# An encoder layer on one core: other landing buffers for the prompt's stored gates and the sample's merged sums, and the eps of the query and key norm as a 65th column

## The chip, the core and the metric

The kernel runs on one core of one Trainium2 chip. The metric is the device time of one execution in microseconds (us). The engines are named as in the profile: PE is TensorE's matrix multiply (PEld its weight load), DVE is VectorE, ACT is ScalarE, POOL is GpSimd, SP is SyncE, from whose queue every transfer of this kernel is issued.

## The reference

One layer of an encoder is applied to two batches with the same weights: a prompt of 512 tokens and a sample of 1024 tokens, 1024 channels each, in float32.

```python
h = rmsnorm(x, norm_g)
qa, ka, va, za, qb, kb, vb, zb, ga, gb = split(h @ w_in)
qa, ka = rmsnorm(qa, qn_a), rmsnorm(ka, kn_a)      # over the 64 of a head
oa = neighbourhood_attention(qa, ka, va, rpb_a) * silu(za)
oa = oa @ w_o_a
qb, kb = rmsnorm(qb, qn_b), rmsnorm(kb, kn_b)
ob = window_gqa_attention(qb, kb, vb, t5_table, sink_b) * silu(zb)
ob = ob @ w_o_b
merged = sigmoid(ga) * oa + sigmoid(gb) * ob
return x + merged @ w_out
```

rmsnorm divides by the root of (mean of squares + eps), with eps 1e-6. Branch A attends on a grid of rows of 64 tokens, branch B in a band of 128 tokens with two key heads, a bias table and a sink.

## The kernel before

**Numbers.** Float32 operands are split into a high part (rounded by ACT, L1172, L605, L665) and a low part (the rest, by DVE or POOL, L1177, L610). A product is three matmuls: high by high, low by high, high by low (L1293, L1294, L1295; in the projection all three at L764). The page calls the parts hh and hl (of h), whi and wlo (of weights), T (of sums), fh and fl (of the weights of filling products).

**Stages.** Each batch passes through `attention_phase` and then `dense_phase`; the profile shows the prompt's attention up to some 220 us, its dense part to 390, the sample's attention to 790, its dense part to the end. In the attention, `project` (L737 and on) multiplies one block of 128 tokens by 384 columns of the input weights, for six groups of columns, 24 matmuls each. Then follows the norm of queries and keys, one chain per product: ACT squares (`sq`, L783), DVE sums over the 64 of each head (`ss`, L788), POOL multiplies by 1/64 and adds eps (`rs_v`, L795), POOL raises to the power -1/2 (`rs_r`, L802), DVE or ACT multiply (`qk`, L819, L669, L665), and PE transposes the result (L864) for the scores (L937). Behind the scores, DVE takes the maximum (L972), ACT the exponential (L981), DVE or POOL the division by the sum (`sb`, L1013 and L1011), PE transposes (L1029) and multiplies by the values (L1066).

`fill_gates` (L1590 and on) gives PE products of the merge gates that can be made at any time of the attention, in the bank "d"; they are the filling products. Their weights land in `fr`, their parts are `fh` and `fl`.

In the dense part the output gates z, the rest of the merge gates, the two branch products and the output product follow. Where it pays, two products share sums of blocks, so that seven products of half size do for eight. For the sample, such sums of h are stored to `t_d`, and such sums of the merged values to `m_d` (`merged_sums`, L1705); `stored_sums` (L1237 to L1253) loads them again (L1245) and splits them into T. The merge loop (L1708 to L1747) makes the branch products, loads the stored gates `g_d` (L1729), multiplies and adds. `pairs_apart` (L1419 to L1505) makes the sample's output product: of every pair it first copies the products that only need h-like operands out of the bank (`leave`, L1440), and later adds those with T.

**Memory.** A landing buffer is a value with a tag; a tag has a number of buffers that are used in turn. For this change: U has 4, ot 2, raw 4, C 4 for the prompt and 5 for the sample, sq 1, and the spare tags fh, fl, fr and w32 (on the page w) 2 each, fc 1.

**What sets the order.** Class `Flow` is a list scheduler that runs when the program is built. Each operation has one or more engines with modelled times, a priority, the operations that it comes after, and the values that it makes or holds. `Flow.run` goes through modelled time, gives each engine the ready operation of the lowest priority number whose buffers are free, and writes the instructions out in that order. For the tags whi, wlo, w32, T, S, raw, U, C and ot a buffer is only given in the order in which the program names its values. On the chip each engine then runs its own list, in that order, with semaphores between engines; SP issues the transfers in its order too, and one that waits for its buffer holds those behind it. So a change of one operation, a buffer or a modelled time moves other instructions as well.

## Time and profile before

| | |
|---|---|
| three runs | 1139.26 us median (1133.87, 1139.26, 1140.91) |
| the profiled execution | 1139.25 us, its span from the first to the last instruction 1137.5 us |
| mean granted clock of TensorE | 0.998 |
| matmuls and transposes | 6079 |
| moved by DMA | 186.11 MB, mean 164 GB/s |
| DVE instructions, POOL instructions | 1988, 438 |

A row of a timeline gives the start in the span, the duration, the engine, the line, the operation, out<-in, and in brackets how long the engine was idle before it and what ended that. A row of the waits gives the engine and line that waited, what it waited for, the total, how often, and the longest. A row of the chain gives the start, the length and what ran, followed back from the last instruction. A window's row gives the busy time of PE, PEld, DVE, ACT and POOL with the number of their instructions, then the granted clock, the DMA engines' busy share and GB/s. Starts of matmuls follow each other faster than their durations, since they are pipelined.

### The profile page before, as it was taken

The page shows a single profiled execution, that of the slowest core. Times are in us where ns is not written, and L with a number is a line of the kernel's source. Part 1 is how long each engine was busy: PE and PEld are TensorE (multiplying, and loading weights), DVE is VectorE, ACT ScalarE, POOL GpSimd, SP SyncE. Part 2 cuts the span into 40 slices and gives each one's busy share as a digit, 9 for nine tenths or more (in the row PEclk, how much of TensorE's full clock was granted, in tenths as well). Part 3 has the DMA queues.
Part 4 walks back from the last instruction along what each step waited for, and adds up shares of the span by engine and source line. Part 5 has one row for each costly group of instructions (what it writes and reads, how often), then busy time and mean ns, then how long its engine had stood idle before and what let it go on. Part 6 is the DMA issues. An engine that isn't in the chain of part 4 may idle for free.

```text
span 1137.5 us, 18703 instructions
## 1 busy us (share of the span) xinstructions
PE 1121.8 (99%) x6079; PEld 975.1 (86%) x6079; DVE 856.8 (75%) x1988; ACT 651.4 (57%) x1499; POOL 339.3 (30%) x438
## 2 busy tenths in 40 slices
PE   8999999999999999999999999999999999999998
PEld 6999988888888889999999988988788888888877
DVE  5878797587776568787878889876988766767564
ACT  5777987644532247565769888877543435333430
POOL 3654433000011144434324343510333323123111
PEclk9999999999999999999999999999999999999999
DMA  7854543488785743121213214244888645756862
GB/s 257 273 159 138 185 115 103 107 254 257 246 286 202 249 138 91 29 61 29 82 41 93 73 38 119 50 131 138 288 261 237 206 158 191 278 197 224 262 208 93
DMA packets 139108, 186.11 MB, mean 164 GB/s; under 512 B 29897, under 2 KB 68561, under 8 KB 139010
## 3 DMA queue, kind: packets, MB, share of 16 engines
q1 hardware_dynamic: 139010, 184.91, 51.8%
q8 instruction: 48, 0.79, 0.3%
q14 instruction: 50, 0.41, 0.1%
HBM read 137.66 MB, written 51.92 MB: 167 GB/s over the span
## 4 chain that ended last, share of the span: by engine, by line
PE 90%; DMA 4%; DVE 2%; ACT 1%; issue 1%; SPq 1%; POOL 0%; ACTq 0%; DVEq 0%
PE p L764 26%; PE x L1293 8%; PE x L1295 8%; PE x L1294 8%; PE x L1066 5%; PE x L1029 5%; PE x L937 5%; PE p L1294 4%; PE p L1295 4%; PE p L1293 4%; PE d L1293 4%; PE d L1295 4%; PE d L1294 4%; PE x L864 2%; DMA w<-in_w_att_dram 1%; DMA U<-m_d 1%
## 5 line engine op out<-in xcount | busy, mean ns | idle before, releaser
L764 PE MATMUL p<-whi,hh 128*128 128x384 f32 x384 | 133.7, 348 | 0.0
L764 PE MATMUL p<-whi,hl 128*128 128x384 f32 x384 | 132.6, 345 | 0.0
L764 PE MATMUL p<-wlo,hh 128*128 128x384 f32 x384 | 132.0, 344 | 0.0
L1172 ACT ACTIVATE whi<-raw 128x512 fp32r<-128x512 f32 (+1 forms) x140 | 81.5, 600 | 73.0 <-PE x L1294 22.5
L981 ACT ACTIVATE sb<-sb,mx 128x384 f32<-128x384 f32 (+1 forms) x192 | 107.7, 565 | 16.9 <-DVE mx L972 16.6
L1294 PE MATMUL x<-T,whi 128*128 128x512 f32 x280 | 108.9, 389 | 0.0
L1293 PE MATMUL x<-T,whi 128*128 128x512 f32 x280 | 108.9, 389 | 0.0
L1295 PE MATMUL x<-T,wlo 128*128 128x512 f32 x280 | 108.9, 389 | 0.0
L764 PE MATMUL p<-whi,hb 128*128 128x384 f32 x384 | 107.6, 346 | 0.0
L1177 DVE TENSOR_TENSOR wlo<-raw,whi 128x512 fp32r<-128x512 f32 (+1 forms) x110 | 73.4, 678 | 34.5 <-ACT whi L1172 31.0
L1177 POOL TENSOR_TENSOR wlo<-raw,whi 128x512 fp32r<-128x512 f32 (+1 forms) x30 | 36.4, 1219 | 210.2 <-ACT whi L1172 210.2
L1040 DVE TENSOR_TENSOR pp<-x,pp 128x512 fp32r<-128x512 f32 (+1 forms) x136 | 82.6, 639 | 19.2 <-ACT pp L1035 18.5
L802 POOL TENSOR_TENSOR rs_r<-rs_v,mhalf 128x4 f32<-128x4 f32 (+1 forms) x72 | 80.7, 1121 | 5.7
L1293 PE MATMUL x<-hh,whi 128*128 128x512 f32 x200 | 78.4, 392 | 2.1 <-ACT fh L1440 2.1
L1035 ACT ACTIVATE pp<-x 128x512 fp32r<-128x512 f32 (+1 forms) x136 | 70.9, 561 | 15.2 <-PE x L1029 14.0
L1295 PE MATMUL x<-hh,wlo 128*128 128x512 f32 x200 | 78.5, 393 | 0.0
L1294 PE MATMUL x<-hl,whi 128*128 128x512 f32 x200 | 78.3, 392 | 0.0
L1066 PE MATMUL x<-pp,v 128*128 128x256 f32 (+1 forms) x368 | 75.8, 322 | 0.0
L764 PEld LDWEIGHTS p<-whi,hl 128*128 128x128 f32 x384 | 72.8, 190 | 1.3 <-issue 1.0
L764 PEld LDWEIGHTS p<-wlo,hh 128*128 128x128 f32 x384 | 73.0, 190 | 1.0 <-issue 0.7
L764 PEld LDWEIGHTS p<-whi,hh 128*128 128x128 f32 x384 | 73.0, 190 | 0.7 <-DVE v L812 0.3
L764 PEld LDWEIGHTS p<-whi,hb 128*128 128x128 f32 x384 | 69.1, 188 | 3.0 <-issue 1.3
(388 smaller groups left out, 2967.8 us busy)
## 6 DMA issues: line engine op xcount, KB each, us to landing
raw<-in_w_g_dram SPq DMA_DIRECT2D x84, 256.0 KB
w<-in_w_att_dram SPq DMA_DIRECT2D x46, 384.0 KB
raw<-in_w_z_dram SPq DMA_DIRECT2D x40, 256.0 KB
ot<-o_d SPq DMA_DIRECT2D x36, 256.0 KB
g_d<-C SPq DMA_DIRECT2D x34, 256.0 KB
fr<-in_w_g_dram SPq DMA_DIRECT2D x28, 256.0 KB
raw<-in_w_out_dram SPq DMA_DIRECT2D x28, 256.0 KB
out_dram<-C SPq DMA_DIRECT2D x19, 256.0 KB
```

The costliest lines, as they stand in the source:

```text
L764: pe.matmul(ps.t[:, :GW], part[u](k), mv.t[:, c], start=k == 0 and m == 0, stop=k == KC - 1 and m == 2,)
L802: lambda e: nc.gpsimd.tensor_tensor(r.t[:, :nn], rv.t[:, :nn], mhalf[:, :nn], op=ALU.pow),
L937: pe.matmul(pss[2 * pair + i].t[:, :width], q.t[rows, u, at : at + P], kv[:, tiles[0] : tiles[-1] + 1 : step], start=n == 0, stop=n == 2,)
L981: act.activation(sb.t[:, :width], sb.t[:, :width], AF.Exp, bias=mx.t[:, i : i + 1], scale=-1.0, accum_out=sm.t[:, i : i + 1],)
L1035: lambda e, pt=pt, pp=pp, nn=nn: act.activation(pp.t[:, 0, :nn], pt.t[:, :nn], AF.Copy),
L1040: lambda e, pt=pt, pp=pp, nn=nn: dve.tensor_tensor(pp.t[:, 1, :nn], pt.t[:, :nn], pp.t[:, 0, :nn].bitcast(F32), op=ALU.subtract),
L1066: pe.matmul(out(), v.t[:, vs], mv(), start=first, stop=last)
L1172: (("act", ACT_(n)),), lambda e: act.activation(hi(), src(), AF.Copy), prio,
L1177: lambda e: engines[e].tensor_tensor(lo(), src(), hi().bitcast(F32), op=ALU.subtract), prio,
L1293: pe.matmul(out, hi.t[:, cs], mh(), start=first and k == 0, stop=False, **more)
L1294: pe.matmul(out, hi.t[:, cs], ml(), start=False, stop=False, **more)
L1295: pe.matmul(out, lo.t[:, cs], mh(), start=False, stop=last and k == len(ws) - 1, **more)
```

## The change

Three edits. First, the tile `sq` is made once per attention phase with 65 columns for each head; POOL writes eps to the 65th column once (L673 of the changed kernel), ACT squares with a scale of 0.125 (0.125 squared is 1/64) into the first 64, DVE sums over 65, and POOL's multiply and add (`rs_v`) is gone: the power takes `ss`. Second, in `stored_sums` the sums of the merged values land in U for even blocks and in ot for odd ones, where all landed in U; those of `t_d` land as before. Third, in the prompt's merge loop the stored gates of branch B land in fh or fl by turns, not in ot, and their transfers come after an earlier product of the loop, or after the sixth last product that reads h.

```diff
@@ -668,6 +668,9 @@
             else:
                 engines[e].tensor_scalar(out, in_, scale, None, op0=ALU.mult)
 
+        sq = tile_([P, 336], F32, "sq", 1)
+        sqv = lambda n: sq.t[:, : n * 65].rearrange("p (h d) -> p h d", d=65)
+        sq_ops = [f.op((("pool", 100),), lambda e: nc.gpsimd.memset(sqv(5)[:, :, 64:], EPS), -0.5, new=[sq])]
         a_tables = geo.tables()
         at = np.cumsum([0, *(n for n, _ in a_tables)]).tolist()
         mask = tile_([P, at[-1]], F32, "mask", 1)
@@ -773,34 +776,25 @@
                         kw["after"].append(done[u, k // 4])
                     o = f.op((("pe", PE_(GW)),), emit, prio, use=[mv], hold=[held[u][k]], **kw)
                     f.begun.setdefault((nt, prio), o)
-            sq = tile_([P, 320], F32, "sq", 1)
             ss = tile_([P, 8], F32, "ss", 2)
-            rv = tile_([P, 8], F32, "rs_v", 2)
             r = tile_([P, 8], F32, "rs_r", 2)
             v = tile_([P, 256], F32R, "v", 7 if nt == NT_S else 6)
             f.op(
                 (("act", ACT_(nn * 64, False)),),
-                lambda e: act.activation(sq.t[:, : nn * 64], ps.t[:, : nn * 64], AF.Square),
-                prio, new=[sq], use=[ps],
-            )
-            f.op(
-                (("dve", DVE_(nn * 64)),),
-                lambda e: dve.tensor_reduce(
-                    ss.t[:, :nn], sq.t[:, : nn * 64].rearrange("p (h d) -> p h d", d=64), axis=AX.X, op=ALU.add
+                lambda e: act.activation(
+                    sqv(nn)[:, :, :64], ps.t[:, : nn * 64].rearrange("p (h d) -> p h d", d=64), AF.Square, scale=0.125
                 ),
-                prio, new=[ss], use=[sq],
-            )
-            f.op(
-                (("pool", 165),),
-                lambda e: nc.gpsimd.tensor_scalar(
-                    rv.t[:, :nn], ss.t[:, :nn], 1.0 / 64, EPS, op0=ALU.mult, op1=ALU.add
-                ),
-                prio, new=[rv], use=[ss],
-            )
+                prio, use=[ps], hold=[sq], after=sq_ops[-1:],
+            )
+            sq_ops.append(f.op(
+                (("dve", DVE_(nn * 65)),),
+                lambda e: dve.tensor_reduce(ss.t[:, :nn], sqv(nn), axis=AX.X, op=ALU.add),
+                prio, new=[ss], hold=[sq], after=f.ops[-1:],
+            ))
             f.op(
                 (("pool", 1000),),
-                lambda e: nc.gpsimd.tensor_tensor(r.t[:, :nn], rv.t[:, :nn], mhalf[:, :nn], op=ALU.pow),
-                prio, new=[r], use=[rv],
+                lambda e: nc.gpsimd.tensor_tensor(r.t[:, :nn], ss.t[:, :nn], mhalf[:, :nn], op=ALU.pow),
+                prio, new=[r], use=[ss],
             )
             nv = GW - nn * 64
 
@@ -1240,7 +1234,7 @@
                 tv[j] = tuple(f.value(tp, [P, 4, nh], F32R, "T", 8) for _ in range(2))
                 vh, vl = tv[j]
                 for k in range(4):
-                    st = spare(("fh", "w32")[k // 2]) if not short and d is t_d and k % 2 else tile_("U", 4)
+                    st = tile_("U", 4) if k % 2 == 0 else spare(("fh", "w32")[k // 2]) if d is t_d else tile_("ot", n_ot)
                     dma(
                         lambda st=st, j=j, k=k: nc.sync.dma_start(st.t[:, :nh], d[j, k]), 512 * nh, prio, new=[st],
                         after=[*after(j, k), *([opened] if d is t_d else [])],
@@ -1705,6 +1699,7 @@
                     lambda vd=vd, j=j: nc.sync.dma_start(m_d[j, k], vd.t), 512 * sn, prio, after=[o], hold=[vd],
                 )
 
+        gates_end = h_reads[-6]
         for q in range(8):
             m = q if short else q // 2 + 4 * (q % 2)
             prio = 12 + q
@@ -1723,8 +1718,11 @@
                     ]
                     m_done[q, n] = product(ps, ws[br], movs, prio, True, True)
                     tag, bufs = (("C", n_c), ("ot", n_ot) if short else ("U", 4))[br]
-                    g = tile_(tag, bufs) if short or br or m < 4 else spare("fl" if n else "fh")
-                    turn = [] if short or br or m < 4 else [m_done[max(q - 2, 0), 0]]
+                    g = spare(("fh", "fl")[m % 2]) if br and short else tile_(tag, bufs) if short or br or m < 4 else spare("fl" if n else "fh")
+                    if short:
+                        turn = [m_done[m - 3, 0] if m > 3 else gates_end] if br else []
+                    else:
+                        turn = [] if br or m < 4 else [m_done[max(q - 2, 0), 0]]
                     dma(
                         lambda g=g, br=br, m=m, n=n: nc.sync.dma_start(g.t, g_d[br, m, :, half[n]]), 512 * nh,
                         prio - 0.5, new=[g], after=[*stores["g", br, m, n], *turn],
```

What the scheduler makes of it, engine by engine, follows at three places (lines of the changed kernel are 2 to 6 lower behind the edits: L1245 is L1239, L1177 is L1171, L802 is L796).

**The sample's merged sums, SP.** Transfers at the end of the sample's branch products and the start of its output product. U and ot are landing buffers, raw holds weights (in_w_out) or stored sums of weights (s_d), C an input or output block. Before:

```order
L1430 DMA raw<-s_d 128x512
L1257 DMA raw<-in_w_out_dram 128x512
L1245 DMA U<-m_d 128x512 x4
L1569 DMA C<-in_xt_s_dram 128x512
L1245 DMA U<-m_d 128x512
L1430 DMA raw<-s_d 128x512
L1583 DMA out_dram<-C 128x512
L1245 DMA U<-m_d 128x512 x3
L1430 DMA raw<-s_d 128x512
L1569 DMA C<-in_xt_s_dram 128x512
L1430 DMA raw<-s_d 128x512
L1245 DMA U<-m_d 128x512 x4
```

In the changed kernel, around the last three stores of m_d:

```order
L1239 DMA U<-m_d 128x512
L1424 DMA raw<-s_d 128x512
L1239 DMA U<-m_d 128x512
L1424 DMA raw<-s_d 128x512
L1239 DMA U<-m_d 128x512 x2
L1699 DMA m_d<-C 128x512
L1699 DMA m_d<-fl 128x512
L1563 DMA C<-in_xt_s_dram 128x512
L1699 DMA m_d<-fh 128x512
L1239 DMA U<-m_d 128x512
```

and some rows further:

```order
L1239 DMA ot<-m_d 128x512
L1251 DMA raw<-in_w_out_dram 128x512
L1239 DMA ot<-m_d 128x512
L1563 DMA C<-in_xt_s_dram 128x512
L1424 DMA raw<-s_d 128x512
L1577 DMA out_dram<-C 128x512
L1424 DMA raw<-s_d 128x512
L1239 DMA ot<-m_d 128x512
L1424 DMA raw<-s_d 128x512
L1239 DMA ot<-m_d 128x512
L1563 DMA C<-in_xt_s_dram 128x512
L1239 DMA ot<-m_d 128x512
```

Before, three loads of m_d stand ahead of its last stores and thirteen behind them. Now eight in U are issued ahead of the last stores or right behind them, one in ot earlier still, and seven in ot later, one by one among other transfers.

**The same place, ACT.** L1440 (now L1434) copies a product out of its bank. Before:

```order
L1440 ACTIVATE fh<-x 128x512
L1172 ACTIVATE T<-U 128x512 x4
L1172 ACTIVATE whi<-raw 128x512 x2
L1172 ACTIVATE whi<-raw 128x256
L1172 ACTIVATE T<-U 128x512 x3
L1440 ACTIVATE fh<-x 128x512
L1172 ACTIVATE T<-U 128x512 x2
```

In the changed kernel:

```order
L1434 ACTIVATE fh<-x 128x512
L1166 ACTIVATE T<-ot 128x512
L1166 ACTIVATE whi<-raw 128x512
L1166 ACTIVATE T<-ot 128x512
L1166 ACTIVATE whi<-raw 128x512
L1166 ACTIVATE whi<-raw 128x256
L1166 ACTIVATE T<-ot 128x512
L1434 ACTIVATE fh<-x 128x512
L1166 ACTIVATE T<-ot 128x512 x2
```

Between the last two copies stood seven splits of sums; three stand there now, the third right ahead of the last copy: it is the split of the fifth of the seven late landings in ot.

**The start of the sample's attention, POOL.** raw<-raw is the end of the prompt's dense part. Before:

```order
L1177 TENSOR_TENSOR wlo<-raw,whi 128x512 x4
L1166 TENSOR_TENSOR raw<-raw 128x512 x4
L1177 TENSOR_TENSOR fl<-fr,fh 128x512
L795 TENSOR_SCALAR rs_v<-ss 128x4
L802 TENSOR_TENSOR rs_r<-rs_v,mhalf 128x4
L795 TENSOR_SCALAR rs_v<-ss 128x4
L802 TENSOR_TENSOR rs_r<-rs_v,mhalf 128x4
L698 TENSOR_TENSOR bias<-mask,raw 128x16x8
```

In the changed kernel:

```order
L1160 TENSOR_TENSOR raw<-raw 128x512
L673 MEMSET sq 128x5
L1160 TENSOR_TENSOR raw<-raw 128x512 x3
L1171 TENSOR_TENSOR fl<-fr,fh 128x512
L796 TENSOR_TENSOR rs_r<-ss,mhalf 128x4 x2
L701 TENSOR_TENSOR bias<-mask,raw 128x16x8
```

The powers stand in the place of the multiply and add, behind the same low part. On PE, six matmuls of filling products (d<-hh,fh and its like) stand there between the projection's matmuls and the first transposes L864, now L858, where nine stood. In the whole program 16 more of the divisions by the sum (L1011) go to POOL.

**The seam between the sample's attention and its dense part, SP.** u_d is the store of gated values, o_d that of attention's output. Before:

```order
L1520 DMA u_d_94<-C 128x512
L1535 DMA ot<-o_d_80 128x8x64 x2
L1520 DMA u_d_94<-C 128x512
L1257 DMA raw<-in_w_z_dram 128x512
L1245 DMA U<-t_d 128x512
L1245 DMA fh<-t_d 128x512
L1245 DMA U<-t_d 128x512
L1257 DMA raw<-in_w_z_dram 128x512
L1245 DMA w_10639<-t_d 128x512
```

In the changed kernel:

```order
L1514 DMA u_d_94<-C 128x512
L1251 DMA raw<-in_w_z_dram 128x512
L1529 DMA ot<-o_d_80 128x8x64
L1251 DMA raw<-in_w_z_dram 128x512 x2
L1239 DMA U<-t_d 128x512
L1239 DMA w_10368<-t_d 128x512
L1239 DMA U<-t_d 128x512
L1239 DMA fh<-t_d 128x512
L1239 DMA U<-t_d 128x512
L1239 DMA w_10392<-t_d 128x512
L1529 DMA ot<-o_d_80 128x8x64
L1514 DMA u_d_94<-C 128x512
```

Six loads of t_d now stand in a row ahead of a store of u_d that stood among them. On PE, 15 more matmuls of filling products stand at the end of the sample's attention, and the first products with T come in whole groups of twelve where they were mixed by threes.

More of the change, by code (lines that the diff above doesn't have):

```diff
@@ L782, in project @@
                 (("act", ACT_(nn * 64, False)),),
[L783 to L799 removed]
+                lambda e: act.activation(
+                    sqv(nn)[:, :, :64], ps.t[:, : nn * 64].rearrange("p (h d) -> p h d", d=64), AF.Square, scale=0.125
+                ),
+                prio, use=[ps], hold=[sq], after=sq_ops[-1:],
+            )
+            sq_ops.append(f.op(
[3 more added lines that the diff above has]
+            ))
             f.op(
                 (("pool", 1000),),
[L802 to L803 removed]
+                lambda e: nc.gpsimd.tensor_tensor(r.t[:, :nn], ss.t[:, :nn], mhalf[:, :nn], op=ALU.pow),
+                prio, new=[r], use=[ss],
             )
```

1 line of the change is left out of this document (removed).

## The prediction

> **What bounds the kernel now.** I read the shares of the engines first, then TensorE's own waits, then windows of 20 us, and last the timeline around each wait.
>
> ```profile
> PE 1121.8 (99%) x6079; PEld 975.1 (86%) x6079; DVE 856.8 (75%) x1988; ACT 651.4 (57%) x1499; POOL 339.3 (30%) x438
> ...
> PE x L1807 <- DMA rb<-in_norm_row_dram: 4.6, 1, 4.6
> PE x L864 <- DVE qk L819: 2.4, 2, 1.9
> PE x L1293 <- ACT fh L1440: 2.1, 1, 2.1
> PE d L1294 <- DVE T L1177: 1.3, 1, 1.3
> ...
> PE p L1294 <- DVE T L1177: 0.2, 1, 0.2
> ```
>
> TensorE is busy for 99% of the span, and no edit takes a matmul away. So an edit can win only what lies between matmuls, or what a lowered clock costs. The list of waits (total, times, longest) is short, and it is the whole stock: the first row is the start of the program, which the change doesn't touch; the other four name the places that the edits can reach.
>
> ```profile
> 220.00:240.00 20.00, 20.00 (x90) 16.54 (x89) 9.28 (x21) 9.21 (x15) 0.00 (x0) 1.00 0.82 245
> 800.00:820.00 20.00, 18.49 (x80) 14.63 (x79) 19.03 (x26) 11.00 (x21) 6.22 (x5) 1.00 0.97 320
> 1080.00:1100.00 20.00, 17.91 (x73) 14.30 (x72) 12.95 (x22) 8.15 (x16) 3.12 (x4) 0.91 0.61 202
> ```
>
> The windows (PE, PEld, DVE, ACT, POOL, each with its instructions, then granted clock, DMA share, GB/s) say the same by place. The prompt's dense part is full. Two windows of the sample's dense part are not: 80 and 73 matmuls where the full one has 90. In the second the mean clock is 0.91.
>
> **The sample's merged sums.** This is the largest term. TensorE's rows around the wait, and the clock behind it:
>
> ```profile
> 1083.27 0.39 PE L1294 MATMUL d<-hl,whi 128*128 128x512 f32 x1
> 1083.50 0.39 PE L1295 MATMUL d<-hh,wlo 128*128 128x512 f32 x1
> 1085.98 0.50 PE L1293 MATMUL x<-hh,whi 128*128 128x512 f32 x1 [2.09 <-ACT fh L1440]
> ...
> 1083.50:1087.10 3.60, 1.51 (x7) 0.94 (x6) 2.12 (x5) 1.64 (x3) 0.00 (x0) 1.00 0.78 290
> 1087.10:1090.50 3.40, 3.40 (x10) 2.67 (x9) 2.31 (x6) 1.90 (x4) 0.00 (x0) 0.52 0.24 90
> ```
>
> From start to start it is 2.48 us, where the matmuls ahead of it follow each other by 0.23: the wait costs 2.25. Then, for 3.40 us, the granted clock is 0.52, which costs 3.40 x 0.48 = 1.6. Together 3.9 us hang on this one place. What ends it is ScalarE's copy L1440, which frees the bank, and that copy stood in ScalarE's queue behind a split of a merged sum:
>
> ```profile
> 1065.07 4.92 DMA U<-m_d
> 1070.01 0.64 ACT T L1172
> ...
> 1074.04 4.59 DMA U<-m_d
> ...
> 1080.04 4.75 DMA U<-m_d
> 1084.83 0.51 issue
> 1085.34 0.59 ACT fh L1440
> ...
> 1088.06 0.63 ACT L1172 ACTIVATE T<-U 128x512 fp32r<-128x512 f32 x1 [1.61 <-DMA U<-m_d]
> ```
>
> The chain of waits shows three rounds of landings, one behind the other, on four buffers U (the last row, from ScalarE's timeline, is the split of the last one). In SyncE's queue the reuse of a U buffer shows directly:
>
> ```profile
> 1065.07 1.91 SPq L1245 DMA_DIRECT2D U<-m_d  x4
> ...
> 1071.39 0.32 SPq L1245 DMA_DIRECT2D U<-m_d  x1
> ```
>
> One round (landing, high part on ScalarE, low part on VectorE, next issue) is 1071.39 - 1065.07 = 6.32 us. In the new order eight landings in U no longer queue for one another's place, and are issued before or right behind the last store of m_d. Seven of the eight in ot are left for the time behind it, on two buffers. I let the first two of them start where the group of four started, at 1065.07, because the same weight load stands beside them. The third and fourth then go at 1071.4, the fifth at 1065.07 + 2 x 6.32 = 1077.7. It is the fifth whose split stands right ahead of the copy on ScalarE. It lands 4.75 later, at 1082.5; its split of 0.64 ends at 1083.1, and the matmul follows 0.64 behind the start of the copy (1085.98 - 1085.34), at 1083.7. Without any wait the matmul would start at 1083.50 + 0.23 = 1083.7. So by the rows the wait is just gone. I leave 0.6 us of it, because two more splits of weights stand between on ScalarE, at about 0.6 each by the row of the split, and one may be in the way. That gives 2.25 - 0.6 = 1.65 for the wait. A stretch with 0.6 us idle instead of 2.25 has 3.0 of 3.6 us busy, and I expect the clock to stay: 1.6 more. **Term: -3.3 us**, bounds 0 and -3.9 (a loss is the first rival). What comes late next is the seventh landing: at 1083.7 or so plus 4.75 it lands at 1088.5, against a last landing in before whose split starts at 1088.06. The matmuls that read that value start three products of twelve matmuls (8.2 us) behind the one at 1085.98's own twelve, so even 3.3 us earlier they have 5 us to spare.
>
> The Trainium skill ("TensorE: Matmul & The Clock Gate", Part 1: The HAM clock gate) puts the fall to half rate behind at least one idle window of about 3.4 us. By that rule a gap of 2.25 us would leave the clock alone, the edit would be worth its wait only, and my sum would be 1.6 us higher, 1136.3. The trace does not agree: 0.52 stands in the row behind a window that was still busy for 1.51 of 3.60 us. I go by the row.
>
> **The eps in the 65th column.** It takes 72 instructions off GpSimd:
>
> ```profile
> L795 POOL TENSOR_SCALAR rs_v<-ss x72: 192/196/1212, 19.9 to 750.5; 128x4 f32<-128x4 f32 x48, 128x5 f32<-128x5 f32 x24
> L788 DVE TENSOR_REDUCE ss<-sq 128x4 f32<-128x256 f32 x48 | 19.7, 411 | 5.1 <-ACT sq L783 4.9
> L1011 POOL TENSOR_TENSOR sb<-sb,rs 128x384 f32<-128x384 f32 x28 | 22.9, 835 | 27.8 <-DVE rs L1005 26.2 <-PE d L1295 1.2 <-PE x L864 0.4
> L1013 DVE TENSOR_SCALAR sb<-sb,rs 128x384 f32<-128x384 f32 x84 | 32.6, 438 | 0.6
> ```
>
> The median is 0.196 us, but GpSimd is 30% busy, and what waits for the chain is TensorE at two places only (L864, 2.4 us in all). The reduce over 65 instead of 64 adds 411 / 64 = 6 ns each, 0.5 us of VectorE in 72, under matmuls. ScalarE's square keeps its size; the strided write has no row here, and I take it as equal: it costs nothing while the chain behind it is hidden, and at most some 0.1 us at each of the two places. Two memsets run long before their use. The freed room also draws 16 of the normalisations L1011 to GpSimd, at 0.835 us against 0.438 on VectorE; the probabilities behind them have matmuls of the projection in front of them, and I count nothing for it, 1 us as the bound.
>
> At the smaller of the two places, 2.4 - 1.9 = 0.5 us, the chain is shorter by 0.196 plus a gap of some 0.08: -0.3. The larger is the start of the sample's attention:
>
> ```profile
> 404.49 1.31 POOL L1177 TENSOR_TENSOR fl<-fr,fh 128x512 fp32r<-128x512 f32 x1 [11.86 <-ACT fh L1172]
> ...
> 404.89 2.10 DVE L667 CAST hb<-hl 128x512 fp32r<-128x512 f32 x2
> ...
> 405.88 1.17 POOL L795 TENSOR_SCALAR rs_v<-ss 128x4 f32<-128x4 f32 x1
> ...
> 407.13 1.01 POOL L802 TENSOR_TENSOR rs_r<-rs_v,mhalf 128x4 f32<-128x4 f32 x1
> ...
> 408.66 0.44 PE L864 MATMUL x<-ident,qk 128*128 128x128 f32 x2 [1.94 <-DVE qk L819]
> ...
> 408.66:413.00 4.34, 4.34 (x26) 4.11 (x27) 3.32 (x13) 1.25 (x4) 1.67 (x3) 1.00 0.19 64
> ```
>
> Here rs_v took 1.17 us instead of 0.196, and ended at 407.05, just behind VectorE's two casts (404.89 + 2.10 = 406.99). In the new order the power stands in its place, behind the same L1177 and beside the same casts. If only the work of rs_v falls away and the hold stays with the power, it gains 0.27; if the hold goes too, 1.25. But six filling matmuls instead of nine now stand ahead of the transposes: TensorE comes 3 x 0.23 = 0.7 us sooner. Net between +0.4 and -0.6; I take 0, nearer to the hold, since the casts have not moved. **Term of the whole edit: -0.3**, bounds +1.5 and -1.
>
> The Trainium skill ("SBUF — State Buffer", SBUF: two separate sides) calls the port pair that VectorE and GpSimd share an exclusive lock, held for a whole instruction. By it the power waits as rs_v did, and the edit gains little here; without it the sum would be lower by about 1 us, 1133.7. The end of rs_v 0.06 us behind the casts agrees with the lock.
>
> **The seam between the sample's attention and its dense part.** No edit aims at it, but the table of orders moves there.
>
> ```profile
> 812.26 0.39 PE L1293 MATMUL d<-T,whi 128*128 128x512 f32 x1
> 813.95 0.50 PE L1294 MATMUL d<-T,whi 128*128 128x512 f32 x1 [1.30 <-DVE T L1177]
> ...
> 810.95 1.27 DVE L1166 TENSOR_TENSOR ot<-ot 128x512 f32<-128x512 f32 x1 [0.43 <-DMA ot<-o_d]
> 812.14 1.75 DVE L1177 TENSOR_TENSOR T<-w,T 128x512 fp32r<-128x512 f32 x1
> ```
>
> The first wait is 813.95 - 812.26 - 0.23 = 1.46 us, the second (0.2 in the list of waits) some 0.4 with its neighbours: 1.8 in all. VectorE, 19.03 of 20 us busy, delivers the parts of the sums late, and one of them is queued behind an addition that waits for a transfer. The new order puts 15 more filling matmuls (15 x 0.23 = 3.4 us) ahead of the first reading of T, and issues six loads of t_d in a row ahead of the store of u_d. The load that waits stays in VectorE's queue, so I take half: **-1.0**, bounds +1 (the weights of w_z come later behind those loads) and -1.8.
>
> **The prompt's stored gates.** They land in four spare buffers instead of two ot.
>
> ```profile
> ACT ot L1513 <- DMA ot<-g_d: 9.9, 6, 2.7
> ```
>
> ScalarE waits 9.9 us for them, but the prompt's dense windows are full (20.00 busy, 220 to 240), and ScalarE is 9.21 of 20 busy there: the wait is under matmuls. Term 0. If that cover were gone, at most its longest wait, 2.7, could show.
>
> **Sum.** -3.3 - 0.3 - 1.0 = -4.6. The profiled execution took 1139.25 us, 1.75 of them outside its span of 1137.5, and stands at the median of the three runs (1139.26; 1133.87 to 1140.91). So 1134.7. The lowest run is 5.4 below the median, as far as my whole gain. A difference under 1%, 11.4 us, is about what measuring this kernel cannot tell from no change.
>
> **Rivals.** (1) The two ot buffers become the chain, and the result is slower. The deciding point is the issue of the fifth late landing: before 1080.04 (the third round of before) the wait shrinks, behind it it grows. In the new order each ot load stands among loads of raw and C and a store of an output, any of which can hold SyncE's queue. A round of 8.5 instead of 6.32 us puts it at 1082.1, 2.1 behind, and a second 3.4 us at half clock would be 1.6 more: 1139.25 + 3.7 - 1.3 of the other terms = 1141.7. For it: one queue issues everything and rounds take over 6 us already. Against it: only seven landings are left, and eight have gone ahead. (2) The copy L1440 then waits for something else of the same age, or the waits only move, and nothing comes of the other terms: 1139. For it: VectorE is at 95% in the seam, and the DMA engines at 0.97 there. (3) The wait goes and the half clock stays, there or at another short gap, because the wait alone did not set it off: the sum without its 1.6, 1136.3. For it: the gap of 1.94 us at 408.66 was followed by 4.34 us at a clock of 1.00. Against it: the fall at 1087.1 comes right behind the longest gap of the dense parts. The rule of the Trainium skill named above would have it so. (4) The change hits the sample's start: 0.7 us less cover in front of L864, a gap of 2.6 instead of 1.94 us, and behind it the clock falls as it did at 1087.1: 0.7 + 1.6 on the forecast, 1137.0. (5) All the waits vanish, with the lower bounds of the terms: 3.9 + 1.8 + 1.0 = 6.7, 1132.5.
>
> **How the numbers follow.** Forecast 0.45 (1133 to 1136.5 of its own), rival 1 0.17, rival 2 0.15, rival 3 0.1, rival 4 0.08, rival 5 0.05. The range reaches past rival 5 and just past rival 1, since the spread of the runs stands on top of each: 1131 to 1142. Faster by over 1% would need under 1127.9, more than all the stock of waits that the edits can reach: 0.03. Slower by over 1%, over 1150.7, would take several new stalls: 0.05. The rest, 0.92, is within 1%.
>
> **What would show it.** Right: in the list of waits the row of L1440 is under 1 us, and the window behind 1080 shows a clock of 1.00; the fifth late ot landing is issued near 1078; the longest wait of L864 stays near 2; the rows of L1294 shrink; the prompt's dense windows stay at 20.00. Wrong: the row of L1440 at 2 or more, or a new releaser such as T from ot; a clock below 1 at 406; new waits for pp or qk in the attention.

## The result, and the profile after

The change made the kernel slower: a median of 1143.28 us (1139.87 to 1149.07, 20 runs) against 1136.28 us (1132.87 to 1141.47, 20 runs). The ratio is 1.0057, with a 95% interval of 1.0045 to 1.0068: 6.5 us, 5.1 to 7.7. I had forecast 4.6 us faster; 1143.28 is just outside the range, which ended at 1142.0. Only the three runs of the section on before were known then, with a median of 1139.26; 20 runs put it 3 us lower. The profiled execution of the changed kernel took 1147.44 us (span 1145.7), that of the kernel before 1139.25; both lie 3 to 4 us above their medians, so the two traces differ by 8.2 us.

The changed kernel's page, busy time of each engine, share of the span and instructions:

```profile
PE 1124.8 (98%) x6079; PEld 976.6 (85%) x6079; DVE 856.9 (75%) x1971; ACT 652.4 (57%) x1502; POOL 320.8 (28%) x382
```

TensorE's waits in it (what waited, for what, total us, times, longest):

```profile
PE x L1805 <- DMA rb<-in_norm_row_dram: 4.5, 1, 4.5
PE x L858 <- DVE qk L813: 4.2, 3, 2.2
PE x L1287 <- ACT hh L1166: 2.2, 1, 2.2
PE x L1023 <- DVE sb L1007: 1.9, 1, 1.9
PE x L1060 <- DVE pp L1034: 1.4, 1, 1.4
PE p L1287 <- ACT whi L1166: 1.1, 1, 1.1
```

The two rows that the prediction wanted gone are gone: the copy behind which a bank waited (L1440, now L1434) and the parts of T (L1294, now L1288). In their place stand waits that the kernel before did not show: for the merged values hh, for a division by the sum of exponentials (L1007), for weighted probabilities (L1034), and more for queries and keys.

The windows say where (PE, PEld, DVE, ACT, POOL, granted clock, DMA share, GB/s):

```profile
120.00:140.00 20.00, 18.14 (x104) 16.35 (x103) 14.74 (x48) 16.19 (x41) 5.09 (x6) 0.91 0.50 168
...
360.00:380.00 20.00, 17.86 (x76) 14.25 (x77) 8.69 (x14) 3.79 (x6) 1.29 (x1) 1.00 0.70 236
...
400.00:420.00 20.00, 17.77 (x87) 16.54 (x86) 11.05 (x22) 8.09 (x14) 4.54 (x5) 0.91 0.80 266
460.00:480.00 20.00, 18.61 (x126) 17.37 (x124) 16.75 (x44) 11.25 (x34) 11.44 (x16) 1.00 0.16 47
800.00:820.00 20.00, 20.00 (x90) 16.57 (x89) 16.44 (x28) 16.30 (x31) 0.00 (x0) 1.00 1.02 359
1080.00:1100.00 20.00, 20.00 (x90) 16.53 (x90) 12.39 (x20) 10.70 (x20) 2.86 (x3) 1.00 0.76 262
```

The two windows that were short of matmuls, 800 and 1080, are full, at 90 matmuls and a clock of 1.00. Four others, of both attention parts and the end of the prompt's dense part, have less busy time than in before, and two of them a clock of 0.91. The same four in before:

```profile
120.00:140.00 20.00, 20.00 (x128) 18.38 (x127) 16.15 (x46) 17.55 (x38) 6.22 (x9) 1.00 0.53 176
...
360.00:380.00 20.00, 20.00 (x90) 16.57 (x89) 11.02 (x17) 3.80 (x6) 2.58 (x2) 1.00 0.65 230
...
400.00:420.00 20.00, 18.07 (x107) 16.81 (x107) 13.20 (x35) 8.28 (x20) 9.92 (x15) 1.00 0.47 159
460.00:480.00 20.00, 19.98 (x133) 19.07 (x132) 15.61 (x48) 9.85 (x29) 8.84 (x16) 1.00 0.14 34
```

Three of them were full; the one of 400 had a gap already, with a clock of 1.00 behind it.

The new order did to one place what the diff doesn't show. Of the changed kernel's timeline, the issue of a load on SyncE's queue and the instructions of ScalarE, VectorE and TensorE near 121 us (start, duration, engine, line, operation, and in brackets the wait just before):

```profile
115.56 0.58 SPq L460 DMA_DIRECT2D xt<-in_x_s_dram  x1
```
```profile
121.38 1.06 ACT L463 ACTIVATE junk<-xt 128x1024 bf16<-128x1024 f32 x1 [1.69 <-DMA xt<-in_x_s_dram]
...
122.43 0.49 ACT L975 ACTIVATE sb<-sb,mx 128x256 f32<-128x256 f32 x1
```
```profile
124.03 0.17 DVE L999 RECIPROCAL rs<-sm 128x2 f32<-128x2 f32 x1 [2.49 <-ACT sb L975]
```
```profile
124.64 0.81 PE L1023 MATMUL x<-ident,sb 128*128 128x128 f32 x4 [1.86 <-DVE sb L1007]
```

and the window behind the gap, as above with the clock third from the end:

```profile
126.20:129.60 3.40, 3.40 (x12) 3.11 (x12) 2.27 (x6) 2.48 (x6) 1.62 (x1) 0.55 0.05 19
```

A square of a block of the sample's input (L463, the seventh block, needed much later) now stands on ScalarE ahead of four of the prompt's exponentials. Its load is issued at 115.56 and lands at 121.4; the exponentials wait behind it, and TensorE waits for them. For 3.4 us behind the gap the clock is 0.55. In the kernel before, the load of the same block was issued at 115.67, and its square stood behind the four exponentials; neither waited:

```profile
117.73 0.49 ACT L981 ACTIVATE sb<-sb,mx 128x256 f32<-128x256 f32 x1
...
123.82 1.09 ACT L463 ACTIVATE junk<-xt 128x1024 bf16<-128x1024 f32 x1
```

### The profile page after: what moved, and what is told of

It reads as the page before. It is cut to its first block, busy times and chain, and to the rows that moved or that the text cites. A ratio compares the mean times of both kernels' runs of the same rounds, so it can differ in the third digit from the quotient of the medians.

```text
span 1145.7 us, 18675 instructions
## 1 busy us (share of the span) xinstructions
PE 1124.8 (98%) x6079; PEld 976.6 (85%) x6079; DVE 856.9 (75%) x1971; ACT 652.4 (57%) x1502; POOL 320.8 (28%) x382
## 4 chain that ended last, share of the span: by engine, by line
PE 85%; DMA 4%; DVE 3%; ACT 2%; issue 2%; POOL 2%; SPq 0%; ACTq 0%; POOLq 0%; DVEq 0%
PE p L767 23%; PE x L1287 8%; PE x L1289 8%; PE x L1288 8%; PE x L1060 5%; PE x L1023 5%; PE x L931 4%; PE d L1287 4%; PE p L1287 4%; PE d L1289 4%; PE p L1289 4%; PE d L1288 4%; PE p L1288 4%; PE x L858 2%; DMA w<-in_w_att_dram 1%
## 5 line engine op out<-in xcount | busy, mean ns | idle before, releaser
L796 POOL TENSOR_TENSOR rs_r<-ss,mhalf 128x4 f32<-128x4 f32 (+1 forms) x72 | 89.3, 1241 | 142.0 <-DVE ss L791 137.5
L1288 PE MATMUL x<-T,whi 128*128 128x512 f32 x280 | 108.9, 389 | 0.0
L1171 DVE TENSOR_TENSOR wlo<-raw,whi 128x512 fp32r<-128x512 f32 (+1 forms) x108 | 72.6, 680 | 36.7 <-ACT whi L1166 34.3
L1171 POOL TENSOR_TENSOR wlo<-raw,whi 128x512 fp32r<-128x512 f32 (+1 forms) x32 | 38.1, 1198 | 218.9 <-DMA t_d<-xt 112.1
L1034 DVE TENSOR_TENSOR pp<-x,pp 128x512 fp32r<-128x512 f32 (+1 forms) x136 | 82.5, 638 | 22.6 <-ACT pp L1029 22.2
L1288 PE MATMUL x<-hl,whi 128*128 128x512 f32 x200 | 78.0, 390 | 0.2 <-DVE hl L1171 0.2
```

Of the source, the lines that this page charges most:

```text
L796: lambda e: nc.gpsimd.tensor_tensor(r.t[:, :nn], ss.t[:, :nn], mhalf[:, :nn], op=ALU.pow),
L1034: lambda e, pt=pt, pp=pp, nn=nn: dve.tensor_tensor(pp.t[:, 1, :nn], pt.t[:, :nn], pp.t[:, 0, :nn].bitcast(F32), op=ALU.subtract),
L1171: lambda e: engines[e].tensor_tensor(lo(), src(), hi().bitcast(F32), op=ALU.subtract), prio,
L1288: pe.matmul(out, hi.t[:, cs], ml(), start=False, stop=False, **more)
```

## The experiments

All times below are against runs of the kernel before on the same chip. The loss could come from the edits' own instructions and buffers, or from the order that they make the scheduler write. The first runs split the change into its edits, and the largest of them into instructions and order.

**The 65th column alone** (the diff's first two pieces, without the buffers).

> The 65th column alone; landing buffers as before. Theory (the order that the scheduler writes for it costs): the trace after the whole change shows new waits in the two attention parts, at 122, 150, 413, 471, 479, 722 and 754 us, and the seam's wait of 1.8 us gone, together about +6: 5 to 7 us slower than before. Rival A (the loss comes from the gates' buffers, by way of the prompt's dense part): within 1.5 us of before. Rival B (only the removed multiply and add shows): 0.5 to 1 us faster.

Measured: 1147.62 us against 1137.91, ratio 1.0077 (1.0056 to 1.0098), 8.8 us slower. The whole loss of the change is in this edit, and more; the theory had its sign and its places, but not the 6.4 us near 360; its 5 to 7 is below the 8.8, though the interval (6.4 to 11.2) reaches into it.

**The sample's merged sums in U and ot alone.**

```diff
-st = spare(("fh", "w32")[k // 2]) if not short and d is t_d and k % 2 else tile_("U", 4)
+st = tile_("U", 4) if k % 2 == 0 else spare(("fh", "w32")[k // 2]) if d is t_d else tile_("ot", n_ot)
```

> The sample's merged sums in U and ot alone; nothing else moves. Theory: the wait behind L1440 at 1083 us and the stretch at half clock go, as in the trace of the whole change: 3 to 4 us faster. Rival (the wait was gone there only because earlier parts had moved): less than 1 us, with a row of L1440 of over 1 us in the list of waits.

Measured: 1135.43 us, ratio 0.998 (0.9969 to 0.999), 2.3 us faster (1.1 to 3.5). TensorE's order is the same matmul for matmul, no wait stands near 1086 us, and the clock there is 1.00. The mechanism holds; the size is below 3 to 4.

**The prompt's stored gates in fh and fl alone** (the diff's last two pieces).

> The prompt's stored gates in fh and fl alone. Theory: the waits at 359 us (2.4 and 0.5) and the longer one at 391 us (1.3 for 0.7) in the trace of the whole change come from this edit: 3 to 4 us slower. Rival (they come from the order that the 65th column makes): within 1 us of before, no wait near 345 to 355 us.

Measured: 1136.91 us, ratio 0.999 (0.9979 to 1.0001), 1.1 us faster, in an interval that still holds no change (2.4 faster to 0.1 slower). My theory for this edit fell: it does not cost 3 to 4 us. It does not cause the waits at 359 us, which the 65th column alone shows without it. The wait at 391 us has its like in this order too: 0.7 us at 385 in before, 1.2 at 386 with both sets of buffers, and none there with the 65th column alone; it differs from one execution to the next.

**The 65th column's instructions in the order of the kernel before.** The scheduler is given a stand-in of 165 ns for the removed instruction, so that nothing else moves; its core:

```diff
+f.op((("pool", 165),), lambda e: None, prio, new=[rv], use=[ss])
 f.op(
     (("pool", 1000),),
-    lambda e: nc.gpsimd.tensor_tensor(r.t[:, :nn], rv.t[:, :nn], mhalf[:, :nn], op=ALU.pow),
+    lambda e: nc.gpsimd.tensor_tensor(r.t[:, :nn], ss.t[:, :nn], mhalf[:, :nn], op=ALU.pow),
```

> The 65th column's instructions (square with a scale into rows of 65, reduce over 65, no multiply and add on GpSimd) in the order of the kernel before: the scheduler is given the old operations and times, so every engine keeps its list, less the 72 removed instructions and with two memsets more. Theory (the instructions cost nothing, the order does): within 1 us of before, rather 0.3 to 0.8 us faster. Rival (the instructions themselves cost, by the strided square or the longer reduce): 3 us or more slower, with new waits of L864 for qk.

Measured: 1142.06 us, ratio 1.0031 (1.0016 to 1.0045), 3.5 us slower. My theory, within 1 us, was wrong here, but the rival's reason hardly shows either: its waits for qk are 3.1 us in all, in before 2.4. One of TensorE's waits is new, for L523 at 30 us (the 1.0 us of this row in before stands elsewhere):

```profile
PE x L535 <- DVE xt L523: 2.8, 1, 2.8
```

GpSimd's and VectorE's timelines there, in the same run:

```profile
24.06 1.52 POOL L806 TENSOR_TENSOR rs_r<-ss,mhalf 128x4 f32<-128x4 f32 x1
25.55 0.36 POOL L708 TENSOR_TENSOR bias<-mask,raw 128x64 f32<-128x64 f32 x1
25.86 1.83 POOL L610 TENSOR_TENSOR wlo<-w,whi 128x768 fp32r<-128x768 f32 x1
```
```profile
24.62 4.51 DVE L708 TENSOR_TENSOR bias<-mask,raw 128x128 f32<-128x128 f32 x10
```

Ten additions of the bias on VectorE take 4.51 us, beside GpSimd's power and low part. In the kernel before they stand like this (VectorE, then GpSimd):

```profile
27.05 1.64 DVE L698 TENSOR_TENSOR bias<-mask,raw 128x128 f32<-128x128 f32 x10
```
```profile
28.83 2.28 POOL L610 TENSOR_TENSOR wlo<-w,whi 128x768 fp32r<-128x768 f32 x1
```

There the ten additions took 1.64 us and were over before GpSimd began the low part. Without rs_v, GpSimd reaches its long instruction before VectorE is through.

The next runs test that, and the order as such.

**The same, with the multiply and add left for the prompt's first products.**

> The 65th column in the order of the kernel before, as in the run that was 3.5 us slower, but for the prompt's first products GpSimd does a multiply and add (by 1, plus 0) again. In that run the list of waits had 2.8 us for L523 at 27 us, behind ten additions of the bias on VectorE that took 4.51 us for 1.64, while GpSimd ran a low part of 1.83 us that started 3 us earlier than before. Theory (the removed instruction lets GpSimd's long instruction run into VectorE's additions at the start, and the rest costs nothing): within 1 us of before. Rival (the square and the reduce cost all along): still 3 us slower.

Measured: 1138.93 us against 1137.44, ratio 1.0009 (0.9994 to 1.0025): no difference that can be told. The ten additions in this run's timeline:

```profile
25.32 1.65 DVE L708 TENSOR_TENSOR bias<-mask,raw 128x128 f32<-128x128 f32 x10
```

So most of the 3.5 us were this collision: four multiply and adds are put back, and with the first of them the additions are at 1.65 again. In the other 68 products the removed instruction, the strided square and the longer reduce cost and gain nothing that shows (0.7 faster to 2.8 slower). The two runs were measured on different chips, and their intervals just overlap.

**The 65th column's order with the multiply and add put back** (the core of the edit).

```diff
+nc.gpsimd.tensor_scalar(rv.t[:, :nn], ss.t[:, :nn], 1.0, 0.0, op0=ALU.mult, op1=ALU.add)
+nc.gpsimd.tensor_tensor(r.t[:, :nn], rv.t[:, :nn], mhalf[:, :nn], op=ALU.pow)
```

> The 65th column alone, in its own order, but GpSimd does a multiply and add (by 1, plus 0) ahead of each power again: the 72 instructions are back, the order stays that of the run with the 65th column alone, which was 8.8 us slower than before. Theory (the order costs, not the instructions): 7 to 11 us slower than before, with the waits of that run, at 122 us for a division behind the exponentials and at the end of the prompt's branch products. Rival (the missing instruction shifts GpSimd's work against VectorE's on the shared port): 4 us slower or less.

Measured: 1147.38 us, ratio 1.0078 (1.0057 to 1.0098), 8.9 us slower, where the same order without the 72 instructions was 8.8. The loss goes with the order, not with the instructions.

**One number of the scheduler's model changed, nothing else.**

```diff
-(("pool", 165),),
+(("pool", 200),),
```

> The kernel before with one number of the scheduler's model changed: the multiply and add on GpSimd is modelled at 200 ns instead of 165. Every instruction and buffer is as before, only the order is another. Theory (before stands at an order that is better than others, and any new order costs): 3 to 12 us slower. Rival (orders differ little, and the loss is bound to what the 65th column does): within 2 us of before.

Measured: 1143.4 us, ratio 1.0041 (1.0027 to 1.0055), 4.7 us slower. The same operations in another order (30 of the divisions by the sum go to GpSimd besides) cost some 70% of what the change cost.

**Both sets of buffers without the 65th column.**

> Both sets of landing buffers without the 65th column. Theory (the two add up, at 2.3 and 1.1 us): 3 to 4 us faster than before. Rival (both runs show only what any small shift of the prompt's dense part brings): 1 to 2 us faster.

Measured: 1134.85 us, ratio 0.9973 (0.9959 to 0.9986), 3.1 us faster: the sum of the two alone, 3.4, is well inside the interval (1.6 to 4.7), whose lower end touches the rival's 1 to 2.

The last runs look for the place, the price and the remedy.

**The square behind the late load.** The seventh block of the sample squares the block before it (sq_of below), so that nothing on ScalarE waits for its load here.

```diff
-lambda e: act.activation(junk.t, xt.t, AF.Square, accum_out=ss.t)
+lambda e: act.activation(junk.t, sq_of.t, AF.Square, accum_out=ss.t)
```

> The 65th column alone in its own order (8.8 us slower than before), but the seventh block of the sample takes its sum of squares from the block before it, which has long landed; so that block's norm is another, and ScalarE's square of it no longer waits for a load. In that run ScalarE waited at 121 us for this load with six exponentials behind it, TensorE waited 1.9 us for the division at 122 us, and the clock was half behind it. Theory (that load in front of the exponentials is one of the places of the loss, worth the wait and the half clock): 5 to 6 us slower than before. Rival (the wait at 122 moves to the next thing that is late): still 8 to 9 us slower.

Measured: 1144.44 us against 1139.42, ratio 1.0054 (1.0034 to 1.0075), 6.2 us slower, just above the 5 to 6 that I gave, and 2.6 less than with the load in front. (Behind that load stand four exponentials, not six.) The intervals of the two ratios overlap, so the size is loose, but the wait (TensorE's waits, 1.9 us in the changed kernel) and the clock behind it (window) are plain in this run's trace:

```profile
PE x L1027 <- DVE sb L1011: 0.3, 1, 0.3
```
```profile
122.00:126.00 4.00, 3.86 (x24) 3.24 (x23) 3.23 (x14) 4.00 (x14) 1.11 (x3) 1.00 1.03 374
```

**The multiply and add done twice, in the order of before.**

> The kernel before with each of the 72 multiply and adds on GpSimd done twice, in the same order. It prices the instruction where it is on the path. Theory (it is on the path only where TensorE waits for queries and keys, and the rest is covered): within 1 us of before, or up to 1.5 us slower. Rival (GpSimd's chain sets the pace of the attention): 4 us slower or more.

Measured: 1139.26 us, ratio 1.0002 (0.9987 to 1.0017). So 72 more of them cost nothing that shows, between 1.5 us faster and 1.9 slower.

**Another order with the 65th column** (the power modelled at 1060 ns instead of 1000).

> The 65th column alone, with the power modelled at 1060 ns for the scheduler instead of 1000; the same instructions in another order. Theory (the loss hangs on the order that happens to come out): a loss clearly other than 8.8 us, anywhere between 0 and 12, with the waits at other places. Rival (the 65th column costs 8 us in any order of its own): 7 to 10 us slower, with the waits at 122, 360 and 480 us.

Measured: 1147.66 us, ratio 1.0077 (1.0056 to 1.0098), 8.8 us slower: the rival's number, with waits at 123, 357, 469 and 477 us. My theory, that the loss would clearly move, is not borne out. This order is not far from the other, though: a comparison of TensorE's lists in the two traces, line by line, has 458 lines that differ, where the 65th column against before has 1206. Whether some order of the column is as good as that of before stays open; one only was tried.

**All three edits with the order held.** The order of the run with both sets of buffers, the column's instructions, and the multiply and add left for the prompt's first four products.

> All three edits, in the order that the scheduler gives for both sets of landing buffers with the old operations, and with the multiply and add (by 1, plus 0) left for the prompt's first products. Theory (the buffers gain 3, the column 0 when the order is held): 1.5 to 3.5 us faster than before, where the change as it is is 6.5 us slower. Rival (the three edits disturb each other): 1 us or more slower than before.

Measured: 1135.33 us against 1139.42, ratio 0.9969 (0.9955 to 0.9983), 3.5 us faster, in the band. The three edits that made the kernel 6.5 us slower make it 3.5 faster when the column does not move the order (and 4 of the 72 multiply and adds stay). Two rows of TensorE's waits in this run, and its window of 1080:

```profile
PE x L873 <- DVE qk L828: 2.4, 3, 1.3
PE d L1303 <- DVE T L1186: 1.3, 1, 1.3
```
```profile
1080.00:1100.00 20.00, 20.00 (x90) 16.57 (x89) 13.84 (x21) 6.80 (x14) 4.17 (x4) 1.00 0.62 191
```

The list has the old small waits again (qk, T), no new one above 0.3 us, and the window of 1080 is full.

TensorE's waits at the places of the loss, in us from start to start of the matmuls above their spacing at full clock, one profiled execution each; where the gap itself ran into the half clock, up to 0.6 us of a figure is the clock's. Places are named by the changed kernel's times. The seam is that between the sample's attention and its dense part:

| | 122 to 126 | 354 to 363 | sample's start | 468 to 483 | 720 to 757 | seam |
|---|---|---|---|---|---|---|
| the kernel before | 0 | 0 | 2.1 | 0.2 | 0 | 1.8 |
| its order, multiply and add done twice | 0 | 5.2 | 2.3 | 1.3 | 0 | 2.1 |
| its order, 65th column, multiply and add left at first | 0 | 2.6 | 2.6 | 0.6 | 0 | 2.3 |
| its order, all three edits | 0 | 0.9 | 1.5 | 0.8 | 0 | 1.9 |
| the change | 2.0 | 2.9 | 2.4 | 2.9 | 1.4 | 0 |
| 65th column alone | 1.9 | 6.4 | 3.0 | 2.8 | 1.4 | 0.3 |
| the column's order, multiply and add back | 1.0 | 4.6 | 2.7 | 1.0 | 1.4 | 0 |
| the column's order, the late load out | 0.3 | 4.9 | 2.6 | 2.9 | 1.5 | 0.3 |

The columns of 122 and 720 are the new order's alone, and that of 468 mostly. Those of 354 and of the sample's start are not: with the prompt's gates in the two ot, the old order had up to 5.2 and 2.6 us there in other executions. The execution of the 65th column alone stood 3.7 us above its median, and in it the clock was at half for three times 3.41 us, 1.7 us lost each; with all three edits in the old order it never was before the last matmul. So the waits and the clock together have the size of the loss, but what each place cost on average is not shown, apart from the late load.

## Why the prediction was wrong

**Failed: the term of the 65th column, -0.3 with bounds +1.5 and -1.** It measured +8.8 (6.4 to 11.2). The step that failed: for all that the new order moves in the two attention parts the sum has one entry, the divisions that the freed room draws to GpSimd ("I count nothing for it, 1 us as the bound"), and everything else there stands at nothing without a reason. Those divisions are not what showed: no row of TensorE's waits in the changed kernel is for GpSimd. I priced the instructions and the two places where TensorE waited for queries and keys. The instructions were priced right: held in order they give no difference but for one collision, and doubled or put back they change nothing. The strided square, which I took as equal, is equal (383 ns on the mean of 48 in both kernels), and the reduce took 4 and 6 ns more, where I had 6. What I did not price is that the edit's modelled times (165 ns less on GpSimd, a longer reduce, a memset) write both attention parts anew, and that waits open in the new order: 2.0 us at 122, 1.4 between 720 and 757, and about 2 more between 468 and 483, with the half clock behind some of them. I had compared the orders at three places and read the rest as even; the square that moved in front of the exponentials stands in ScalarE's order, and would have been found there. No rival had this mechanism; the nearest were the "several new stalls", at 0.05, and in the last paragraph their mark, new waits for pp or qk in the attention.

**Right: the mechanism of the merged sums.** The wait and the half clock are gone in the changed kernel. The fifth late landing, on which the first rival's decision hung, was issued at 1090.05 in the changed kernel, on SyncE's queue, ahead of the copy on ScalarE that the second half waits for:

```profile
1090.05 0.32 SPq L1239 DMA_DIRECT2D ot<-m_d  x1
```
```profile
1093.39 0.60 ACT L1434 ACTIVATE fh<-x 128x512 f32<-128x512 f32 x1
```

TensorE reaches the matmul ahead of that copy's reader 12.2 us later than in before (1095.68 for 1083.50, follow-up at 0.23 us), so this is 1077.9 in the time of before; I had 1077.7. That close an agreement is luck: by the same subtraction the first late landing was issued at 1066.5, where I had 1065.07, and the two rounds took 6.7 and 4.6 us (1078.68, 1085.42, 1090.05), where I had 6.32 for both. (The seventh landing, by my own rounds, is issued at 1065.07 + 3 x 6.32 = 1084.0, not at 1083.7; nothing hangs on it.) The first rival, the ring of two buffers as the new chain, is out.

**Mis-sized: its -3.3.** Alone it measured -2.3 (1.1 to 3.5). The 2.25 us and the stretch at half clock stood in one execution that was 3 us above the median. In other executions with the same products in the same order the wait is 1.1 (the gates' run), 1.5 (the column in the order of before), 0.6 (the same with the multiply and add left at first) and 0.3 (the doubled instruction), and the clock behind it does not fall. The three runs of before spread over 7 us; I took the one trace for the mean.

**Right, at its lower bound: the seam.** I took half of 1.8; the changed kernel has none of it. It came with the same order that cost the rest: the 65th column alone has 0.3 there, and the runs in the order of before have 1.8 to 2.9. That the 15 more filling matmuls ahead of T are the reason is argued, not shown.

**Wrong in its reason: the gates at 0.** I read "full windows" and concluded cover. In the trace of before that was so; in others of the same order the last merged values come late: 1.1 us with the merged sums alone, 2.6 with the column in the old order and the multiply and add left at first, 5.2 with the doubled instruction. The windows of that last run, with the columns as above:

```profile
356.33:359.85 3.52, 0.40 (x2) 0.00 (x1) 2.22 (x5) 0.63 (x1) 0.75 (x1) 1.00 0.83 287
359.85:363.30 3.45, 3.30 (x7) 2.33 (x8) 1.96 (x3) 0.63 (x1) 0.00 (x0) 0.54 0.75 199
```

TensorE is idle for most of 3.5 us and then runs at 0.54. The last gate of that ring of two is issued at 348.90, for 344.03 in before. With the gates' own buffers it is at 339.2 (the gates alone), and the waits are 0.9, 0.9 and 0.5 us in the three runs with this edit and the rest of the order as in before (the gates alone, all three edits, both sets of buffers). That these waits explain the whole 1.1 us is argued, not shown.

**The start of the sample's attention.** The power in the place of the multiply and add was held, as its nearer bound had it. In the changed kernel's timeline, VectorE, GpSimd and TensorE:

```profile
412.98 1.91 DVE L667 CAST hb<-hl 128x512 fp32r<-128x512 f32 x2
```
```profile
413.82 1.41 POOL L796 TENSOR_TENSOR rs_r<-ss,mhalf 128x4 f32<-128x4 f32 x1
```
```profile
415.74 0.52 PE L858 MATMUL x<-ident,qk 128*128 128x128 f32 x2 [2.23 <-DVE qk L813]
```

and the window behind the gap:

```profile
416.50:420.00 3.50, 3.50 (x14) 3.50 (x13) 1.72 (x7) 0.42 (x2) 1.20 (x2) 0.59 0.25 80
```

The power took 1.41 us for 1.01, and the gap grew by 0.3 us (2.40 for 2.11). The clock then fell to 0.59 in this window, which is rival 4, at 1.4 us on top (1.7 by the last section's window); it was one of several losses and not the cause. It did not come with the longer gap alone: with the 65th column alone the gap there was 3.0 us, and the clock stayed at 1.00.

## What to carry to other kernels

Where a scheduler writes the order, price an edit twice: once in the old order (a stand-in of the same modelled time keeps it there), and once for the order itself, by changing one modelled number and nothing else. Here the edits were worth -3.5 us in the old order and the new order some 10 more (+6.5 against -3.5), and a change of 35 modelled ns in the scheduler alone cost 4.7. A wait in one profiled execution is a sample, and before it is counted as a gain, a second trace of the same order is worth more than a finer reading of the first.

## What the runs showed of the hardware that was not expected

The hold on GpSimd beside VectorE moved from the instruction that was removed to the one behind it. Over all 72, in the groups of instructions of the changed kernel (busy us and mean ns of one behind the bar):

```profile
L796 POOL TENSOR_TENSOR rs_r<-ss,mhalf 128x4 f32<-128x4 f32 x48 | 56.1, 1169 | 103.8 <-DVE ss L791 103.7
L796 POOL TENSOR_TENSOR rs_r<-ss,mhalf 128x5 f32<-128x5 f32 x24 | 33.3, 1386 | 38.2 <-DVE ss L791 33.8 <-DVE v L806 4.4
```

The powers took 56.1 + 33.3 = 89.4 us for 80.7 in before, so of the 25.3 us of the removed rows 8.7 came back. Some 6 of these 8.7 are the hold itself, as two pairs with one order each show: 86.5 for 80.7 with the column in the order of before, and 89.4 for 83.2 in the column's order without and with the multiply and add. This agrees with the lock that the Trainium skill ("SBUF — State Buffer", SBUF: two separate sides) describes.

The half clock does not follow from the length of a gap. It fell behind gaps of 2.25 us (before, 1083), 2.03 (the change, 122) and 2.40 (the change, 413), and did not fall behind 2.11 (before, 406) and 2.41 (the change, 359). What tells them apart is where the gap lies. In each trace a stretch at half clock behind a gap lasts 3.41 us, or twice that, at 0.50 (the rows above with 0.54 to 0.59 were cut a few tenths of a us off it), and the stretches of one trace start a whole number of 3.413 us apart: in the changed kernel at 125.83 and 415.96, which is 85 of them, and in before at 1087.21 and, behind the last matmuls, at 1138.41, which is 15. Cut by this grid, the changed kernel's windows at its three gaps and behind them are (columns as above):

```profile
122.42:125.83 3.41, 1.55 (x11) 0.98 (x10) 1.72 (x8) 3.41 (x15) 0.75 (x2) 1.00 0.95 348
125.83:129.24 3.41, 3.41 (x12) 3.12 (x12) 2.53 (x7) 2.49 (x5) 1.62 (x1) 0.50 0.08 32
...
357.94:361.35 3.41, 1.60 (x8) 0.98 (x6) 2.51 (x4) 0.25 (x1) 1.12 (x2) 1.00 0.84 299
361.35:364.77 3.42, 2.76 (x11) 2.04 (x12) 1.98 (x3) 1.01 (x2) 0.00 (x0) 1.00 0.65 198
412.55:415.96 3.41, 1.18 (x8) 0.66 (x6) 3.04 (x7) 2.53 (x4) 2.65 (x2) 1.00 0.92 320
415.96:419.38 3.42, 3.42 (x13) 3.42 (x12) 2.26 (x10) 0.63 (x2) 1.61 (x2) 0.50 0.34 116
```

The gaps at 122 and 413 leave TensorE 1.55 and 1.18 us busy in one window, and the next runs at 0.50; so a window need not be idle throughout. The longest of the three gaps lies across two windows, 1.60 and 2.76 us busy, and the clock stays. Over the fourteen traces, from 20 us on, half clock followed all 15 windows of this grid with up to 1.55 us busy, four of the seven between 1.6 and 1.81, and none with more. The grid lies elsewhere in each execution: its first whole window starts at 1.77 us in the trace of before and at 2.95 in that of the change. So a gap of 2 to 2.4 us costs another 1.7 us (half the clock for 3.41 us) or nothing, and the same order can pay it in one execution and not in the next. The Trainium skill ("TensorE: Matmul & The Clock Gate", Part 1: The HAM clock gate) gives a free-running window of 3413 ns. The 3.41 us of the half clock and the grid agree with it.
